# Mixer of a two-layer encoder: rows of ones and gates beside q and k placed by DMA, and q and k taken out of PSUM in one pass

## Chip, core and metric

The kernel runs on one core of a Trainium2 chip. The metric is the time of one execution on the device in microseconds (us), median of three runs; lower is better. The profiled execution is a run of its own. PE is TensorE, ACT is ScalarE, DVE is VectorE, POOL is GpSimd, and SP is the engine that issues most DMAs.

## What is computed

The reference is an encoder trunk of two layers over 256 time steps of 1024 features, in float32. Each layer is a half-step SwiGLU feed-forward network (FFN), a mixer, and a second FFN. What matters here is the attention branch of the mixer:

```python
h = rms_norm(x, g_mix[l]);  z = h @ w_in[l]            # z holds q, k, v, f_logit, gates, ...
qn = rms_norm(q, g_q)                                   # per head of 64; 16 heads
kn = rms_norm(k, g_k)
cum = cumsum(log_sigmoid(f_logit + b_forget), over time)
s = qn @ kn.T * 64 ** -0.5 + cum[query] - cum[key]      # causal
o = softmax(s) @ v
```

The other branch is a gated linear recurrence (RG-LRU); both are gated, added, multiplied by `w_o` and added to x.

## The kernel before

**Matrix products.** Every large product is done in three passes, because each float32 weight is split into a high part (`whi`, a cast on ACT, line 324) and a low part (`wlo`, a subtraction on DVE, line 333). Weights stream from DRAM in pieces of 512 KB (`raw`, five buffers, issued by SP). One visit of a piece multiplies two slices of 128 rows; for each slice there are three matmuls of 512 columns (lines 364 to 366). The two blocks of 128 time steps (`tok` 0 and 1) are worked off one after the other, so an accumulator of 128x512 is complete after eight slices, 24 matmuls.

**Order.** The order of all instructions is fixed when the program is built. A planner `S` keeps a clock of planned time for each engine and a list of chains (generators). After each slice, which it counts as 3 x (512/2400 + 0.0027) = 0.648 us, it calls a hook in which chains whose due time has come put their next instructions into the engines' queues. `yield t, "d"` means: not before planned time t, unless DVE's own planned clock is already further. On the chip each engine executes its queue strictly in order and waits on semaphores. POOL's queue holds the few POOL operations and POOL's DMA issues.

**PSUM.** There are two x banks, two y banks and four z banks. A big product of the mixer takes its accumulator from the x banks (`xbank`), transposes and scores use z banks, and the attention output uses y banks.

**q and k.** The 16 heads are in two halves (`hf`), and each half has a block for q (`w` = 0) and one for k (`w` = 1), in the order q0, k0, q1, k1. When an accumulator is complete, `ev_qk` scales it by the row's inverse norm into `nat` in SBUF (`scale_any`, line 459 on DVE or 462 on ACT, whichever the planner holds to be free sooner) and squares it on ACT (line 1029). `qk_chain` then reduces the squares per head on DVE (line 874), takes the power -1/2 on POOL (line 878), multiplies `nat` by it on DVE (line 881), transposes the result on PE (`quad`, line 448) and scales it into the tile `qk[w, hf]`.

**Extra rows.** That tile has two planes (`e`, even and odd heads) of 128 partitions. In each plane 64 partitions hold the head's features; two groups of 32 of the other 64 hold extra features, so that one matmul of 128 rows gives the scores with the gate terms added. One group selects the head with ones (`new_qk`, a POOL copy of a part of the identity matrix, line 901), the other holds the cumulated gates `cum` (`bias_chain`, copies on DVE, line 308, or ACT, line 311). A group of ones in the tile of q meets a group of gates in the tile of k, and the other way round.

**Attention.** `att_chain` starts eight pairs of heads, at most two at a time. It starts pairs 0 to 3 when the four chains of half 0 are over and `bias_chain(0)` has been planned, and pairs 4 to 7 likewise for half 1. A pair does its scores on PE (line 934), masks and takes minima on DVE (line 950), exponentials on ACT (line 959), scaling (lines 459 and 462), transposes (line 448), copies out of PSUM (lines 308 and 311), and the product with v (line 992). All this is woven between the matmuls of k0, q1, k1 and the gate blocks.

Of the kernel before, what the change touches and what calls it, by code (L numbers as in the profile page):

```python
# [8 lines left out]
F32 = mybir.dt.float32  # L9
F32R = mybir.dt.float32r  # L10
AF = mybir.ActivationFunctionType
ALU = mybir.AluOpType
AX = mybir.AxisListType

P = 128
D = 1024
KD = D // P
T = 256
# [4 lines left out]
DH = 64  # L23
# [128 lines left out]
def act_c(n, ap=0):  # L152
    return 0.11 + 0.000833 * n + 0.093 * ap


def dve_c(n):
    return 0.09 + 0.00104 * n
# [3 lines left out]
def hybrid_encoder_kernel(  # L161
# [6 lines left out]
    nc = tc.nc  # L168
    S = Sched()
# [7 lines left out]
    tmp_p = ctx.enter_context(tc.tile_pool(name="tmp", bufs=NTMP))  # L177
    att_p = ctx.enter_context(tc.tile_pool(name="att", bufs=NLIVE))
    sm_p = ctx.enter_context(tc.tile_pool(name="sm", bufs=2))
    ps_x = ctx.enter_context(tc.tile_pool(name="ps_x", bufs=2, space=bass.MemoryType.PSUM))  # L180
    ps_y = ctx.enter_context(tc.tile_pool(name="ps_y", bufs=2, space=bass.MemoryType.PSUM))
    ps_z = ctx.enter_context(tc.tile_pool(name="ps_z", bufs=4, space=bass.MemoryType.PSUM))
# [3 lines left out]
    def nm(s):  # L186
        cnt[0] += 1
        return f"{s}_{cnt[0]}"

    def new(pool, shape, tag, dt=F32):  # L190
        return pool.tile(shape, dt, tag=tag, name=nm(tag))

    nat_ring, z_ring, y_ring, tmp_ring = [], [], [], []

    def new_nat(n=512):
        r = S.claim(nat_ring, NNAT)
        return new(nat_p, [P, n], "nat"), r

    def new_tmp(shape=None):
        r = S.claim(tmp_ring, NTMP)  # L200
        return new(tmp_p, shape or [P, 512], "tmp"), r

    def bank(pool, tag):
        return pool.tile([P, 512], F32, tag=tag, name=nm(tag))
# [11 lines left out]
    def slot(shape, dt=F32):  # L216
        i = free_slots.pop(0)
        t = slot_p.tile(shape, dt, tag=f"s{i}", name=nm(f"s{i}"))
        return [t, i]

    def free(s):
        free_slots.append(s[1])
        s[0] = None
# [4 lines left out]
    def bc(ap, n):  # L228

        return ap.unsqueeze(2).to_broadcast([ap.shape[0], ap.shape[1], n])  # L230
# [72 lines left out]
    def copy_any(out_, in_, n, dep, fast=False):  # L303

        a = max(S.t["a"], dep, S.now) + act_c(n)
        d = max(S.t["d"], dep, S.now) + dve_c(n if not fast else n // 2)
        if d < a:
            nc.vector.tensor_copy(out_, in_)
            S.t["d"] = d
        else:  # L310
            nc.scalar.copy(out_, in_)
            S.t["a"] = a
        return min(a, d) + LAT
# [65 lines left out]
    def take(n):  # L379
        i = hpos[0]  # L380
        hpos[0] += n
        return i

    def block(lhs, evac, pool, ncol=512, norm=None, mixed=False):

        nk = 1024 // ncol
        n = KD // nk
        i0 = take(n)
        accs = {}
        order = [(tok, i) for tok in range(NT) for i in range(n)]  # L390
        if mixed:
            order = [(tok, i) for i in range(n) for tok in range(NT)]
        for tok, i in order:
            if i == 0:
                a, r = pool()
                accs[tok] = a[:, :ncol], r
            acc, r = accs[tok]

            def fin():
                evac(tok, acc)  # L400
                r.free = True

            if norm is not None:
                norm.before(tok, i * nk)
            visit(i0 + i, acc, lhs, i * nk, tok, i == 0, i == n - 1, fin if i == n - 1 else None)


    ident = const.tile([P, P], F32, name="ident")
# [45 lines left out]
    def scale_any(out_, in_, scale, n, fast=False):  # L454

        a = max(S.t["a"], S.now) + act_c(n, 1)
        d = max(S.t["d"], S.now) + dve_c(n if not fast else n // 2)
        if d < a:
            nc.vector.tensor_scalar(out=out_, in0=in_, scalar1=scale, scalar2=None, op0=ALU.mult)
            S.t["d"] = d  # L460
        else:
            nc.scalar.activation(out_, in_, AF.Copy, scale=scale)
            S.t["a"] = a
        return min(a, d) + LAT
# [80 lines left out]
    def rs(tok):  # L545
        return rstd[:, tok:tok + 1]

    def xbank():
        r = Rec()
        return bank(ps_x, "x"), r  # L550


# [61 lines left out]


    fw = {}

    def load_fw(l):
        r, rr = new_tmp([P, KD, H])
        nc.sync.dma_start(out=r, in_=w_in[l, :, OFF_F:OFF_F + H].rearrange("(k p) n -> p k n", p=P))  # L620
        w = const.tile([P, KD, 2 * H], F32R, tag="fw", name=nm("fw"))
        fw[l] = w
        yield S.now + 8.0, "a"
        nc.scalar.copy(w[:, :, :H], r)
        yield S.use("a", 0.4), "d"
        nc.vector.tensor_tensor(out=w[:, :, H:], in0=r, in1=f32(w[:, :, :H]), op=ALU.subtract)
        S.use("d", 0.3)
        rr.free = True
# [25 lines left out]
    def mix(l, nrm):  # L654
        lhs = nrm.lhs()
# [81 lines left out]
        cum = att_p.tile([P, T], F32, tag="cum", name=nm("cum"), bufs=1)  # L737
# [130 lines left out]
        qk = {}  # L868
        qk_c = {0: [], 1: []}

        def qk_chain(w, hf, tok, nat, sq, dep):
            yield dep, "d"
            rq = sm_p.tile([P, 8], F32, tag="rq", name=nm("rq"), bufs=4)
            nc.vector.tensor_reduce(out=rq, in_=sq[0].rearrange("p (h d) -> p h d", d=DH), axis=AX.X, op=ALU.add)
            sq[1].free = True
            nc.vector.tensor_scalar(out=rq, in0=rq, scalar1=1.0 / DH, scalar2=EPS, op0=ALU.mult, op1=ALU.add)
            d = S.use("d", dve_c(512) + 0.1)
            nc.gpsimd.tensor_tensor(out=rq, in0=rq, in1=mhalf, op=ALU.pow)
            yield d + POW, "d"
            n3 = nat[0].rearrange("p (h d) -> p h d", d=DH)  # L880
            nc.vector.tensor_tensor(out=n3, in0=n3, in1=bc(rq, DH), op=ALU.mult)
            yield S.use("d", dve_c(512)), "p"
            ps, rz = zbank()
            quad(nat[0], ps)
            nat[1].free = True
            gcol = gqm[:, l:l + 1] if w == 0 else col(R_GK)
            for e in range(2):
                yield S.now, "d"
                b = slice(e * DH, e * DH + DH)
                scale_any(qk[w, hf][0][b, e, :, tok * P:(tok + 1) * P], k4(ps)[b], gcol[b], 512)  # L890
            rz.free = True

        def quarters(w):

            return [(e, slice(r, r + 32), slice(r ^ 32, (r ^ 32) + 32)) for e, r in ((0, 64 + 32 * w), (1, 32 * w))]

        def new_qk(w, hf):
            t = qk[w, hf] = slot([P, 2, KD // 2, T])
            for e, one, _ in quarters(w):
                c0 = one.start + hf * 8 + e  # L900
                nc.gpsimd.tensor_copy(t[0][one, e], bc(ident[one, c0:c0 + 7:2], T))

        def bias_chain(hf):
            for w in range(2):
                for e, _, acc in quarters(w):
                    yield S.now, "d"
                    n = KD // 2
                    copy_any(qk[w, hf][0][acc, e], cum[acc].unsqueeze(1).to_broadcast([32, n, T]), n * T, S.now, True)


        OT = {}
# [109 lines left out]
        for hf in range(2):  # L1021
            for w in range(2):
                new_qk(w, hf)

                def ev_qk(tok, acc):
                    nat = new_nat()
                    scale_any(nat[0], acc, rs(tok), 512)
                    sq = new_tmp()
                    nc.scalar.activation(sq[0], acc, AF.Square, scale=rs(tok))
                    dep = S.use("a", act_c(512, 1))  # L1030
                    c = S.add(qk_chain(w, hf, tok, nat, sq, dep), dep, "d")
                    nat[1].user = sq[1].user = c
                    S.step(c)
                    qk_c[hf].append(c)
                block(lhs, ev_qk, xbank)
            if hf == 0:
                att = S.add(att_chain(), S.now, "p", True)

# [2 lines left out]
        for gi in range(2):  # L1041
            g = slot([P, NT, D])
            gates.append(g)
            for hf in range(2):
                c0 = gi * D + hf * 512
# [86 lines left out]
    def rows_chain():  # L1132
        yield 20.0, "p"
        for l in range(L):
            load_rows(l)
        yield S.now + 70.0, "p"
        for l in range(L):
            ps, rz = zbank()
            nc.tensor.transpose(ps[:, :NROW], rows[:, l, :], ident[:NROW, :NROW])
            yield S.use("p", 0.12), "d"  # L1140
            nc.vector.tensor_copy(cols[:, l, :], ps[:, :NROW])
            nc.vector.tensor_scalar(out=gqm[:, l:l + 1], in0=cols[:, l, R_GQ:R_GQ + 1], scalar1=-(DH ** -0.5),
                                    scalar2=None, op0=ALU.mult)
            S.use("d", 0.3)
            rz.free = True
        free(rows_s)
        yield from load_fw(0)

    def program():
# [75 lines left out]
```

## Time and profile before

| | |
|---|---|
| median of 3 runs | 1305.29 us (1305.26 to 1306.33) |
| the profiled execution: its own time | 1305.66 us |
| its span, first to last instruction | 1303.9 us |
| PE busy | 1287.2 us (99%) |
| DVE / ACT / POOL busy | 815.5 / 706.5 / 84.8 us |
| granted TensorE clock, mean | 1.000 of full speed |

Times in the rows are microseconds from the first instruction unless marked ns. A matmul's record lasts from its issue to the modelled end of its pipeline, so matmuls of 0.39 us overlap and follow each other every 0.23 us. In a timeline, "x4" means four instructions merged, and the bracket gives the idle time of the engine before the row and what ended it. A helper's line stands for all its callers: line 448 is every group of transposes.

### The profile page before, as it was taken

The page shows a single profiled execution, that of the slowest core. Times are in us where ns is not written, and L with a number is a line of the kernel's source. Part 1 is how long each engine was busy: PE and PEld are TensorE (multiplying, and loading weights), DVE is VectorE, ACT ScalarE, POOL GpSimd, SP SyncE. Part 2 cuts the span into 40 slices and gives each one's busy share as a digit, 9 for nine tenths or more (in the row PEclk, how much of TensorE's full clock was granted, in tenths as well). Part 3 has the DMA queues.
Part 4 walks back from the last instruction along what each step waited for, and adds up shares of the span by engine and source line. Part 5 has one row for each costly group of instructions (what it writes and reads, how often), then busy time and mean ns, then how long its engine had stood idle before and what let it go on. Part 6 is the DMA issues. An engine that isn't in the chain of part 4 may idle for free.

```text
span 1303.9 us, 16570 instructions
## 1 busy us (share of the span) xinstructions
PE 1287.2 (99%) x6209; PEld 1065.9 (82%) x6209; DVE 815.5 (63%) x1131; ACT 706.5 (54%) x988; POOL 84.8 (7%) x85
## 2 busy tenths in 40 slices
PE   8999999999999999999999999999999999999998
PEld 6888888887778888888888888888877788888887
DVE  5655558799765666555575555678987567655553
ACT  6544446776865455444454444558768554544442
POOL 5000001005100000000000000000250000000000
PEclk9999999999999999999999999999999999999999
DMA  8655557365446565555565565574654455555551
GB/s 273 198 188 184 181 161 217 123 191 154 118 142 201 181 194 194 184 182 183 162 208 183 192 194 182 156 212 126 181 146 145 145 195 172 189 190 192 192 186 59
DMA packets 128896, 229.92 MB, mean 176 GB/s; under 512 B 9848, under 2 KB 22320, under 8 KB 128816
## 3 DMA queue, kind: packets, MB, share of 16 engines
q1 hardware_dynamic: 127968, 228.75, 55.6%
q8 instruction: 49, 0.80, 0.2%
q0 software_dynamic: 832, 0.11, 0.1%
q14 instruction: 31, 0.25, 0.1%
q10 hardware_dynamic: 16, 0.00, 0.0%
HBM read 227.78 MB, written 1.05 MB: 175 GB/s over the span
## 4 chain that ended last, share of the span: by engine, by line
PE 91%; DVE 6%; ACT 1%; issue 1%; DMA 1%; SPq 0%; DVEq 0%; ACTq 0%
PE x L364 13%; PE x L365 13%; PE x L366 13%; PE z L364 12%; PE z L366 12%; PE z L365 12%; PE z L448 4%; PE y L364 3%; PE y L366 3%; PE y L365 3%; DVE wlo L333 2%; PE z L934 1%; PE z L762 1%; PE y L992 1%; DVE s L824 1%
## 5 line engine op out<-in xcount | busy, mean ns | idle before, releaser
L333 DVE TENSOR_TENSOR wlo<-raw,whi 128x1024 fp32r<-128x1024 f32 x424 | 515.9, 1226 | 251.2 <-ACT whi L324 243.2
L324 ACT CAST whi<-raw 128x1024 fp32r<-128x1024 f32 x424 | 442.4, 1050 | 319.9 <-PE z L366 136.8
L364 PE MATMUL x<-whi,s 128*128 128x512 f32 x832 | 337.3, 405 | 1.5 <-ACT whi L324 1.3
L365 PE MATMUL x<-wlo,s 128*128 128x512 f32 x832 | 325.3, 391 | 1.9 <-DVE wlo L333 1.1
L366 PE MATMUL x<-whi,s 128*128 128x512 f32 x832 | 325.3, 391 | 0.1
L364 PE MATMUL z<-whi,s 128*128 128x512 f32 (+1 forms) x752 | 282.5, 376 | 0.0
L366 PE MATMUL z<-whi,s 128*128 128x512 f32 (+1 forms) x752 | 279.7, 372 | 0.0
L365 PE MATMUL z<-wlo,s 128*128 128x512 f32 (+1 forms) x752 | 279.6, 372 | 0.0
L366 PEld LDWEIGHTS x<-whi,s 128*128 128x128 f32 x832 | 156.3, 188 | 34.1 <-DVE s L471 0.5
L364 PEld LDWEIGHTS x<-whi,s 128*128 128x128 f32 x832 | 156.5, 188 | 33.7 <-issue 2.1
L365 PEld LDWEIGHTS x<-wlo,s 128*128 128x128 f32 x832 | 156.7, 188 | 32.4 <-DVE wlo L333 2.0
L366 PEld LDWEIGHTS z<-whi,s 128*128 128x128 f32 x752 | 141.8, 189 | 24.9
L365 PEld LDWEIGHTS z<-wlo,s 128*128 128x128 f32 x752 | 141.9, 189 | 23.7
L364 PEld LDWEIGHTS z<-whi,s 128*128 128x128 f32 x752 | 141.8, 189 | 23.7
L589 ACT ACTIVATE nat<-z,rstd 128x512 f32<-128x512 f32 (+1 forms) x46 | 30.0, 653 | 77.7 <-PE z L366 77.6
L364 PE MATMUL y<-whi,s 128*128 128x512 f32 x176 | 71.0, 403 | 0.0
L366 PE MATMUL y<-whi,s 128*128 128x512 f32 x176 | 68.9, 391 | 0.0
L365 PE MATMUL y<-wlo,s 128*128 128x512 f32 x176 | 68.7, 391 | 0.0
L594 DVE SCALAR_TENSOR_TENSOR nat<-z,rstd,nat 128x512 f32<-128x512 f32 (+1 forms) x48 | 33.8, 704 | 54.2 <-PE z L366 54.2
L469 ACT CAST s<-z 128x512 fp32r<-128x512 f32 (+1 forms) x56 | 31.1, 555 | 66.9 <-PE z L448 66.5
L501 POOL TENSOR_TENSOR rstd<-msum,mhalf 128x1 f32<-128x1 f32 x12 | 11.8, 985 | 819.4 <-ACT whi L324 524.5
L471 DVE TENSOR_TENSOR s<-z,s 128x512 fp32r<-128x512 f32 (+1 forms) x56 | 36.4, 650 | 29.7 <-ACT s L469 29.7
(152 smaller groups left out, 933.7 us busy)
## 6 DMA issues: line engine op xcount, KB each, us to landing
raw<-in_w_up_dram SPq DMA_DIRECT2D x176, 512.0 KB, 4.6
raw<-in_w_in_dram SPq DMA_DIRECT2D x112, 512.0 KB, 4.3
raw<-in_w_down_dram SPq DMA_DIRECT2D x88, 512.0 KB, 4.4
raw<-in_w_lru_out_dram SPq DMA_DIRECT2D x16, 512.0 KB, 4.7
raw<-in_w_attn_out_dram SPq DMA_DIRECT2D x16, 512.0 KB, 4.7
raw<-in_w_o_dram SPq DMA_DIRECT2D x16, 512.0 KB, 5.3
tmp<-in_b_gate_dram SPq DMA_DIRECT2D x8, 256.0 KB, 4.9
xn<-in_x_dram SPq DMA_DIRECT2D x4, 256.0 KB, 4.6
```

The lines of the kernel that those rows point to most:

```text
L324: nc.scalar.copy(hi, raws[i])
L333: nc.vector.tensor_tensor(out=lo, in0=raws.pop(i), in1=f32(hi), op=ALU.subtract)
L364: nc.tensor.matmul(acc, lhsT=lhs(0, k0 + kk)[:, ts], rhs=hi[:, kk, :], start=st, stop=False)
L365: nc.tensor.matmul(acc, lhsT=lhs(0, k0 + kk)[:, ts], rhs=lo[:, kk, :], start=False, stop=False)
L366: nc.tensor.matmul(acc, lhsT=lhs(1, k0 + kk)[:, ts], rhs=hi[:, kk, :], start=False, stop=sp)
L448: nc.tensor.transpose(dst_ps[:, j * P:(j + 1) * P], src[:, j * P:(j + 1) * P], ident)
L469: nc.scalar.copy(hi, t)
L471: nc.vector.tensor_tensor(out=lo, in0=t, in1=f32(hi), op=ALU.subtract)
L589: nc.scalar.activation(s[tok][0], acc, AF.Silu, scale=rs(tok))
L594: nc.vector.scalar_tensor_tensor(out=h, in0=acc, scalar=rs(tok), in1=h, op0=ALU.mult, op1=ALU.mult)
L762: nc.tensor.matmul(ps[:, g, :], lhsT=wax[0][:, g, n, :], rhs=xr[0][:, n, :], start=True, stop=True)
L824: nc.vector.tensor_tensor_scan(t_[:, n, :], r[:, n, :], i_[:, n, :], 0.0, ALU.mult, ALU.add)
```

## The change

The POOL copies of ones become DMA loads, issued by POOL, from two images (`ones_d`) in DRAM; these are built once, at the end of the chain that prepares constants in the first FFN (`ones_chain`). The copies of gate rows become DMAs from the tile `cum`, issued by POOL, and the chain lets 3.0 us of planned time pass. The scaling into `nat` in `ev_qk` is dropped; `qk_chain` keeps the accumulator's PSUM bank until the power is there, and one DVE instruction multiplies by both factors on the way out. The banks become a ring of two records (`x_ring`), so that the planner knows when a bank is held; k of half 0 takes the y banks.

```diff
--- before.py
+++ after.py
@@ -177,6 +177,7 @@
     tmp_p = ctx.enter_context(tc.tile_pool(name="tmp", bufs=NTMP))
     att_p = ctx.enter_context(tc.tile_pool(name="att", bufs=NLIVE))
     sm_p = ctx.enter_context(tc.tile_pool(name="sm", bufs=2))
+    dram = ctx.enter_context(tc.tile_pool(name="dram", bufs=1, space=bass.MemoryType.DRAM))
     ps_x = ctx.enter_context(tc.tile_pool(name="ps_x", bufs=2, space=bass.MemoryType.PSUM))
     ps_y = ctx.enter_context(tc.tile_pool(name="ps_y", bufs=2, space=bass.MemoryType.PSUM))
     ps_z = ctx.enter_context(tc.tile_pool(name="ps_z", bufs=4, space=bass.MemoryType.PSUM))
@@ -190,7 +191,8 @@
     def new(pool, shape, tag, dt=F32):
         return pool.tile(shape, dt, tag=tag, name=nm(tag))
 
-    nat_ring, z_ring, y_ring, tmp_ring = [], [], [], []
+    nat_ring, z_ring, y_ring, x_ring, tmp_ring = [], [], [], [], []
+    held = [None]
 
     def new_nat(n=512):
         r = S.claim(nat_ring, NNAT)
@@ -397,8 +399,8 @@
             acc, r = accs[tok]
 
             def fin():
-                evac(tok, acc)
-                r.free = True
+                held[0] = r
+                r.free = evac(tok, acc) is None
 
             if norm is not None:
                 norm.before(tok, i * nk)
@@ -546,7 +548,7 @@
         return rstd[:, tok:tok + 1]
 
     def xbank():
-        r = Rec()
+        r = S.claim(x_ring, 2)
         return bank(ps_x, "x"), r
 
 
@@ -614,6 +616,26 @@
 
 
     fw = {}
+    ones_d = [dram.tile([P, 2, KD // 2, T], F32, name=f"ones_d{hf}") for hf in range(2)]
+
+    def quarters(w):
+
+        return [(e, slice(r, r + 32), slice(r ^ 32, (r ^ 32) + 32)) for e, r in ((0, 64 + 32 * w), (1, 32 * w))]
+
+    def ones_chain():
+
+        for hf in range(2):
+            t = slot([P, 2, KD // 2, T])
+            for w in range(2):
+                for e, one, _ in quarters(w):
+                    c0 = one.start + hf * 8 + e
+                    yield S.now, "a"
+                    nc.scalar.copy(t[0][one, e], bc(ident[one, c0:c0 + 7:2], T))
+                    S.use("a", act_c(4 * T))
+            for e in range(2):
+                b = slice((1 - e) * DH, (2 - e) * DH)
+                nc.gpsimd.dma_start(out=ones_d[hf][b, e], in_=t[0][b, e])
+            free(t)
 
     def load_fw(l):
         r, rr = new_tmp([P, KD, H])
@@ -868,7 +890,7 @@
         qk = {}
         qk_c = {0: [], 1: []}
 
-        def qk_chain(w, hf, tok, nat, sq, dep):
+        def qk_chain(w, hf, tok, acc, r, sq, dep):
             yield dep, "d"
             rq = sm_p.tile([P, 8], F32, tag="rq", name=nm("rq"), bufs=4)
             nc.vector.tensor_reduce(out=rq, in_=sq[0].rearrange("p (h d) -> p h d", d=DH), axis=AX.X, op=ALU.add)
@@ -877,8 +899,11 @@
             d = S.use("d", dve_c(512) + 0.1)
             nc.gpsimd.tensor_tensor(out=rq, in0=rq, in1=mhalf, op=ALU.pow)
             yield d + POW, "d"
-            n3 = nat[0].rearrange("p (h d) -> p h d", d=DH)
-            nc.vector.tensor_tensor(out=n3, in0=n3, in1=bc(rq, DH), op=ALU.mult)
+            nat = new_nat()
+            h3 = lambda t: t.rearrange("p (h d) -> p h d", d=DH)
+            nc.vector.scalar_tensor_tensor(out=h3(nat[0]), in0=h3(acc), scalar=rs(tok), in1=bc(rq, DH), op0=ALU.mult,
+                                           op1=ALU.mult)
+            r.free = True
             yield S.use("d", dve_c(512)), "p"
             ps, rz = zbank()
             quad(nat[0], ps)
@@ -890,22 +915,16 @@
                 scale_any(qk[w, hf][0][b, e, :, tok * P:(tok + 1) * P], k4(ps)[b], gcol[b], 512)
             rz.free = True
 
-        def quarters(w):
-
-            return [(e, slice(r, r + 32), slice(r ^ 32, (r ^ 32) + 32)) for e, r in ((0, 64 + 32 * w), (1, 32 * w))]
-
         def new_qk(w, hf):
             t = qk[w, hf] = slot([P, 2, KD // 2, T])
             for e, one, _ in quarters(w):
-                c0 = one.start + hf * 8 + e
-                nc.gpsimd.tensor_copy(t[0][one, e], bc(ident[one, c0:c0 + 7:2], T))
+                nc.gpsimd.dma_start(out=t[0][one, e], in_=ones_d[hf][one, e])
 
         def bias_chain(hf):
             for w in range(2):
                 for e, _, acc in quarters(w):
-                    yield S.now, "d"
-                    n = KD // 2
-                    copy_any(qk[w, hf][0][acc, e], cum[acc].unsqueeze(1).to_broadcast([32, n, T]), n * T, S.now, True)
+                    nc.gpsimd.dma_start(out=qk[w, hf][0][acc, e], in_=cum[acc].unsqueeze(1).to_broadcast([32, KD // 2, T]))
+            yield S.now + 3.0, "d"
 
 
         OT = {}
@@ -1023,16 +1042,16 @@
                 new_qk(w, hf)
 
                 def ev_qk(tok, acc):
-                    nat = new_nat()
-                    scale_any(nat[0], acc, rs(tok), 512)
+                    r = held[0]
                     sq = new_tmp()
                     nc.scalar.activation(sq[0], acc, AF.Square, scale=rs(tok))
                     dep = S.use("a", act_c(512, 1))
-                    c = S.add(qk_chain(w, hf, tok, nat, sq, dep), dep, "d")
-                    nat[1].user = sq[1].user = c
+                    c = S.add(qk_chain(w, hf, tok, acc, r, sq, dep), dep, "d")
+                    r.user = sq[1].user = c
                     S.step(c)
                     qk_c[hf].append(c)
-                block(lhs, ev_qk, xbank)
+                    return c
+                block(lhs, ev_qk, ybank if w > hf else xbank)
             if hf == 0:
                 att = S.add(att_chain(), S.now, "p", True)
 
@@ -1144,6 +1163,7 @@
             S.use("d", 0.3)
             rz.free = True
         free(rows_s)
+        yield from ones_chain()
         yield from load_fw(0)
 
     def program():
```

## Rows read from the trace of the kernel before

**Rows 1.** Page, part 1: busy us, share of the span, instructions per engine.
```profile
span 1303.9 us, 16570 instructions
...
PE 1287.2 (99%) x6209; PEld 1065.9 (82%) x6209; DVE 815.5 (63%) x1131; ACT 706.5 (54%) x988; POOL 84.8 (7%) x85
```

**Rows 2.** Stretches of the first mixer: us, busy us per engine, PEclk, DMA share, GB/s.
```profile
285.00:303.00 18.00, 17.12 (x81) 13.94 (x80) 17.90 (x22) 13.58 (x17) 7.98 (x5) 1.00 0.63 179
303.00:329.00 26.00, 24.25 (x118) 19.84 (x117) 21.95 (x46) 18.49 (x35) 14.25 (x8) 1.00 0.50 146
329.00:357.00 28.00, 26.58 (x155) 20.34 (x154) 22.04 (x54) 24.34 (x56) 4.19 (x2) 1.00 0.42 123
...
312.50:314.70 2.20, 0.47 (x3) 0.06 (x2) 2.09 (x5) 2.15 (x3) 1.41 (x1) 1.00 0.16 61
```

**Rows 3.** Waits of PE: us in total, times, longest us.
```profile
PE z L934 <- DVE s L308: 3.5, 2, 1.7
```

**Rows 4.** Timeline around the first stall: start, us, engine, line, operation, [idle before].
```profile
295.90 1.23 DVE L333 TENSOR_TENSOR wlo<-raw,whi 128x1024 fp32r<-128x1024 f32 x1
...
297.55 3.60 POOL L901 COPY s<-ident 32x1024 f32<-32x1024 f32 x2
...
298.18 2.06 DVE L333 TENSOR_TENSOR wlo<-raw,whi 128x1024 fp32r<-128x1024 f32 x1
...
301.83 0.63 PE L448 MATMUL z<-ident,nat 128*128 128x128 f32 x4 [0.88 <-DVE nat L881]
```

**Rows 5.** Timeline around the second stall.
```profile
310.97 0.60 PE L448 MATMUL z<-ident,nat 128*128 128x128 f32 x4
...
312.28 0.67 DVE L874 TENSOR_REDUCE rq<-tmp 128x8 f32<-128x512 f32 x1
...
313.18 2.10 DVE L308 COPY s<-cum 32x1024 f32<-32x1024 f32 x3
313.29 2.07 POOL L878 TENSOR_TENSOR rq<-rq,mhalf 128x8 f32<-128x8 f32 x1 [0.88 <-DVE rq L876]
...
314.71 1.61 PE L934 MATMUL z<-s,s 128*128 128x128 f32 x8 [1.75 <-DVE s L308]
```

**Rows 6.** Timeline of the third stall and of half 1.
```profile
340.85 1.64 POOL L878 TENSOR_TENSOR rq<-rq,mhalf 128x8 f32<-128x8 f32 x1 [6.77 <-DVE rq L876]
...
350.24 0.55 PE L448 MATMUL z<-ident,pr 128*128 128x128 f32 x3 [1.11 <-ACT pt L311]
...
353.72 1.47 PE L934 MATMUL z<-s,s 128*128 128x128 f32 x8
```

**Rows 7.** Groups of instructions by shape: busy us, mean ns | idle before.
```profile
L311 ACT COPY s<-cum 32x1024 f32<-32x1024 f32 x6 | 6.3, 1043 | 0.1
```

**Rows 8.** POOL's DMA issues, lines 439 and 434: ns min/median/max; issue to landing.
```profile
L439 POOL DMA_DIRECT2D bfb<-in_b_forget_dram x2: 573/573/573, 26.4 to 33.7; - x2
...
DMA to landing us min/median/max: 3.2/3.8/5.2
```

**Rows 9.** Timeline: the bank's chain in half 1.
```profile
325.84 1.64 POOL L878 TENSOR_TENSOR rq<-rq,mhalf 128x8 f32<-128x8 f32 x1 [7.07 <-DVE rq L876]
...
327.04 0.75 DVE L459 TENSOR_SCALAR nat<-x,rstd 128x512 f32<-128x512 f32 x1 [1.34 <-PE x L366]
...
329.96 0.69 DVE L881 TENSOR_TENSOR nat<-nat,rq 128x512 f32<-128x512 f32 x1
```

**Rows 10.** Page, part 6: DMA issues, KB each, median us to landing.
```profile
out_dram<-xn SPq DMA_DIRECT2D x4, 256.0 KB, 2.0
```

**Rows 11.** Chain that ended last, in order of time: start, us, what.
```profile
302.46 0.23 PE x L364
```

**Rows 12.** Stretches after PE's last matmul, columns as in rows 2.
```profile
1300.00:1301.00 1.00, 0.20 (x1) 0.00 (x0) 0.69 (x1) 0.00 (x0) 0.00 (x0) 1.00 0.00 0
...
1303.00:1303.90 0.90, 0.00 (x0) 0.00 (x0) 0.00 (x0) 0.00 (x0) 0.00 (x0) 0.63 0.00 0
```

**Rows 13.** Timeline of PE at the start.
```profile
1.43 2.39 PE L1162 MATMUL x<-ident 128*128 128x128 f32 x10 [1.43 <-POOL ident masks.py:199]
```

## Prediction

> **What bounds the kernel now.** I read the page first: TensorE (PE) is busy in 99% of the span [rows 1]. So the kernel can only gain where PE stands still, 1303.9 - 1287.2 = 16.7 us in all. Next came the table of stretches, to see where that is: in the first mixer PE is idle for 0.88, 1.75 and 1.42 us in three neighbouring stretches, 4.05 us together [rows 2], and the second layer repeats it. The other 8.6 us lie at the start and the end, far from the change. That gives a ceiling: an edit that removed every mixer stall would save 2 x 4.05 = 8.1 us, 0.6%. VectorE (DVE) is busy 17.9 of 18 us in the first of these stretches and looks like the bound, but PE is busy in 17.12 of the same 18. Work taken from DVE or ScalarE (ACT) counts only through those three stalls.
>
> The list of waits names what PE waited for, each entry twice, once per layer; the longest is the first scores behind the copies of the gate rows [rows 3]. The timelines show why each stall happens.
>
> *First stall.* While GpSimd (POOL) copies the rows of ones (line 901), a DVE subtraction that took 1.23 us just before takes 2.06. The multiplication of line 881 behind it ends late, and PE waits 0.88 us for it [rows 4].
>
> *Second stall.* After the last transposes of half 0 (at 310.97), DVE reduces the next block's squares, then makes three of the four gate-row copies; POOL takes the power for that next block at 313.29. The scores were next on PE at 314.71 - 1.75 = 312.96 and start at 314.71 [rows 5].
>
> *Third stall.* Transposes wait 1.11 us for an ACT copy out of PSUM [rows 6], which stands in ACT's queue behind softmax scalings and a weight cast.
>
> **The change, part by part, per layer.**
>
> *Rows of ones.* Eight POOL copies, 3.6 us for the pair in the first stall [rows 4], become eight POOL DMA issues. An issue of 128 pieces takes 0.57 us [rows 8], a pair 1.1, and nothing in these rows shows an issue slowing DVE. The first stall goes: -0.88 us (bounds -0.88, and 0 if issues hold DVE as copies do). The source in DRAM is made once, by eight ACT copies of 32x1024, 8 x 1.04 = 8.3 us [rows 7], in the first FFN; ACT is idle 46% of the span [rows 1], so nothing. Without that cover each would delay a weight cast by up to 1.04 us, 8.3 once. The traffic is some 5 MB on DMA engines that are busy 63% at most in the three stretches [rows 2].
>
> *One pass out of PSUM.* Eight scalings (0.75 us on DVE) disappear; the multiplication now reads PSUM and does both, for which I take the 0.75 of the scaling in place of its own 0.69 [rows 9]. That frees 8 x 0.75 - 8 x 0.06 = 5.5 us of DVE and ACT, worth something only in the third stall.
>
> *Gate rows.* Eight copies, about 0.7 us on DVE and 1.04 on ACT [rows 5, 7], become eight POOL DMAs, and the code lets 3.0 us of planned time pass before the scores may be issued. When do the four issues of half 0 run? POOL executes in program order, and the power of the next block (line 878) is ahead of them: the reduction that feeds it stands before the copies on DVE [rows 5]. It ends at 313.29 + 2.07 = 315.36, 4.4 us after the transposes began. The third issue (k, even heads) is the last that the first score needs and starts 4.4 + 2 x 0.57 = 5.5 us after them. The trace shows no such transfer. The nearest are small POOL DMAs into SBUF with the DMA engines full, 3.2/3.8/5.2 us from issue to landing [rows 8], and 256 KB out of SBUF on idle engines, 2.0 [rows 10]. DMA is only 16% busy around this stall [rows 2], so I take 2.7, nearer the low end; bounds 2.0 and 5.2. Landing: 8.2 us after the transposes began (7.5 to 10.7).
>
> When does PE ask? Before the change, 2.0 us after them. The 3.0 planned us are 3.0/0.648 = 4.6 steps of three matmuls (the code counts 0.648 for one), and a step takes 3 x 0.23 = 0.69 us [rows 11]: 3.2 more. So PE asks at 5.2, a step earlier or later by where the planner's hook falls, and waits 8.2 - 5.2 = 3.0 us where it waited 1.75: +1.25 (bounds 7.5 - 5.9 - 1.75 = -0.1 and 10.7 - 4.5 - 1.75 = +4.5). Everything on PE is late behind it, since PE executes in order.
>
> The Trainium skill, "DMA: Bandwidth & Descriptors", section "Anatomy of one DMA — SWDGE (gpsimd) path", fits a DMA issued by POOL as about 2.0 us plus its bytes over 436 GB/s, so 2.3 us for 128 KB. By that estimate the wait would be 2.6 and the sum 0.8 us lower over both layers; no row here shows a transfer of this kind.
>
> In half 1 the same four issues have no power left ahead of them: the last one starts at 340.85 and takes 1.64, and the scores of half 1 begin at 353.72 [rows 6]. The issues need only the slot and the gate rows, so they land at about 342.5 + 3 x 0.57 + 2.7 = 346.9: hidden by some 7 us of PE work. If that cover were gone, they would cost what half 0 does.
>
> *Third stall.* With DVE free of its scalings, more softmax scalings go there from ACT. I count 1.0 of the 1.42 us in this stretch as gained (0 to 1.42).
>
> *Held banks.* A bank now stays occupied through square, reduction, power and multiplication. Two x banks alternate, and the y banks serve only k of half 0, so at four places (half 1 and the first gate block) an accumulation waits if the chain of the bank's last user outlasts the accumulation between. Tight is the second block of half 1: in the trace the power ends at 325.84 + 1.64 = 327.48, and with 0.75 for the product the bank would be free at 328.2, while the accumulation between is done by 327.04 [rows 9]. PE would wait 1.2 there; at the other places the accumulation between shares PE with scores and products and lasts longer. Less DVE work ahead shortens the chain: I take +0.8, bounds 0 and 3.6 (the product ended at 329.96 + 0.69 = 330.65).
>
> *Sum.* -0.88 + 1.25 - 1.0 + 0.8 = +0.17 per layer, +0.3 for two. The profiled execution took 1305.66 us (span 1303.9 and 1.8 around it), so 1306.0; the median of the runs is 0.4 below that execution: **1305.6**. All low ends give 2 x (-0.88 - 0.1 - 1.42) = -4.8, all high ends 2 x (4.5 + 3.6) = +16.
>
> **Rivals.**
>
> *A: the scores don't wait.* If the planner places the four issues ahead of that power, they run some 4 us earlier and are there in time. Then -0.88 - 1.75 - 1.0 + 0.8 = -2.8 per layer, -5.7 in all: 1299.6. For it: the planner's order hangs on due times that all move a little. Against: the reduction and power are planned before the gate rows now, and no edit moves them behind. Chance 0.24.
>
> *B: the clock falls in the stall (slower).* At the end of the kernel, where PE's last work is over at 1300.2, the granted clock still stood at 1.00 in the first microsecond and averaged 0.63 in the last 0.9, while stalls of up to 1.75 us left it at 1.00 [rows 2, 12]. A fall comes about 3 us into an idle stretch, as long as the forecast wait. At the lower of the two levels (1.2 GHz) PE works half as fast: at the start ten transposes took 2.39 us, 0.24 each, against 0.15 [rows 5, 13]. If it lasts about as long as the idle stretch, 3 us, it loses 1.5 us; with a wait of 3.5, past the point, that is +2.0 per layer: 1305.6 + 4.0 = 1309.6. Against: 3.0 is just short of it. Chance 0.15.
>
> The Trainium skill, "TensorE: Matmul & The Clock Gate", section "What's actually happening", says the same of an idle array: half the clock, and back after it has been busy. By that rule, the trace agrees.
>
> *C: late landing or long-held banks.* Landing after 3.8 us, the median with full engines, adds 1.1 per layer (1307.8); a bank wait of 2.0 instead of 0.8 adds 1.2 (1308.0); both, 1310.2. For it: reduction and product wait in DVE's queue behind subtractions of 1.2 us. Against: DVE loses over 5 us of work. Chance 0.21.
>
> **Numbers.** The forecast has 0.40, with a range of its own from 1303 to 1308. A measurement here tells about 0.2%, 2.6 us, from no change: 1302.7 to 1307.9 counts as the same. A lies on the faster side, B and most of C on the slower; the forecast spills little: faster 0.26, same 0.40, slower 0.34. To leave out no more than two in ten the range takes in A's time and B and C with one bound more: 1299.5 to 1311.
>
> **What would show it.** Right: subtractions at 1.2 us throughout the mixer; PE waiting about 3 us for a gate-row DMA before the first scores of each layer and not at the fifth head pair; the four issues after the power on POOL; no wait of 0.88 us before transposes. Wrong: scores released by something else; a granted clock under 1.00 inside the mixer; PE waiting over 2 us for the product at the start of an x accumulation; idle time of PE in a mixer well off 4.2 us.

## Result and the profile after

The changed kernel takes **1314.47 us** (median of 6 runs, 1314.18 to 1315.44) where the kernel before takes 1305.28 beside it (6 runs, 1304.72 to 1306.33): a ratio of 1.0071, interval 1.0061 to 1.0081. It is 0.7% slower. The forecast of 1305.6 and its range to 1311 both missed, on the slow side.

The profiled execution took 1314.18 us against 1305.66 before. Its page, part 1, has the columns of [rows 1]:

```profile
span 1312.1 us, 16582 instructions
...
PE 1289.5 (98%) x6209; PEld 1067.7 (81%) x6209; DVE 806.4 (61%) x1121; ACT 700.6 (53%) x974; POOL 79.1 (6%) x105
```

The span grew by 8.2 us. PE stood still for 1312.1 - 1289.5 = 22.6 us instead of 16.7, which is +5.9, and was busy for 2.3 us more with the same 6209 matmuls, so part of them ran slower. DVE lost 9.1 us of work, ACT 5.9 and POOL 5.7, and nothing of that shows in the time.

The list of PE's waits (us in total, times, longest) tells where it stood. The entry of [rows 3], 3.5 us for DVE copies, has this in its place:

```profile
PE z L953 <- DMA s<-cum: 12.4, 5, 5.5
...
PE z L450 <- DVE nat L904: 1.5, 2, 0.7
```

The scores (now line 953) wait for the gate-row DMAs, 12.4 us in all. The same three stretches as in [rows 2] show that the first stall has shrunk from 0.88 to 0.73 us, the second has grown from 1.75 to 5.52, and the third, 1.42 us, is gone. The granted clock is no longer 1.00 throughout:

```profile
285.00:303.00 18.00, 17.27 (x81) 14.06 (x80) 17.30 (x23) 12.48 (x15) 7.58 (x5) 1.00 0.62 183
303.00:329.00 26.00, 20.48 (x91) 16.33 (x89) 16.36 (x34) 12.34 (x15) 10.63 (x12) 0.87 0.70 201
329.00:357.00 28.00, 28.00 (x161) 21.94 (x160) 19.07 (x51) 19.78 (x54) 5.50 (x6) 1.00 0.36 100
```

The timeline of the second stall answers to [rows 5]:

```profile
310.46 0.60 PE L450 MATMUL z<-ident,nat 128*128 128x128 f32 x4
...
311.77 0.67 DVE L896 TENSOR_REDUCE rq<-tmp 128x8 f32<-128x512 f32 x1
...
312.79 1.66 POOL L900 TENSOR_TENSOR rq<-rq,mhalf 128x8 f32<-128x8 f32 x1 [3.45 <-DVE rq L898]
...
314.42 2.26 POOL L926 DMA_DIRECT2D s<-cum  x4
...
321.11 1.62 PE L953 MATMUL z<-s,s 128*128 128x128 f32 x4 [5.23 <-DMA s<-cum]
...
323.02 1.62 PE L953 MATMUL z<-s,s 128*128 128x128 f32 x4 [0.29 <-DMA s<-cum]
```

The order is the one forecast: transposes at 310.46, reduction, power on POOL, then the four issues at 314.42. PE runs dry at 321.11 - 5.23 = 315.88. The first scores need the third issue, at about 315.6, and start at 321.11: 5.5 us from that issue to use. The view of the issuing lines, from 310 to 320 us, gives how long transfers took from issue to landing (lowest, median, highest), first for the gate rows, then for the weight pieces that SP issues:

```profile
L926 POOL DMA_DIRECT2D s<-cum x4: 550/556/615, 314.4 to 316.1; - x4
...
DMA to landing us min/median/max: 2.3/5.4/6.8
```

```profile
L302 SPq DMA_DIRECT2D raw<-in_w_in_dram x3: 368/368/368, 314.9 to 317.8; - x3
...
DMA to landing us min/median/max: 4.8/6.8/7.0
```

The first gate-row transfer landed in 2.3 us, as estimated, and the later ones took 5 to 7. Three weight pieces of 512 KB are issued in the same 3 us. Stretches inside the stall (columns as in [rows 2]) show what the DMA engines and the clock did:

```profile
316.00:318.00 2.00, 0.00 (x0) 0.00 (x0) 2.00 (x4) 1.54 (x2) 0.68 (x2) 1.00 0.89 168
...
315.88:319.17 3.29, 0.00 (x0) 0.00 (x0) 2.71 (x5) 1.62 (x2) 1.20 (x3) 1.00 0.94 210
319.17:321.11 1.94, 0.00 (x1) 0.04 (x1) 0.00 (x0) 0.00 (x0) 1.94 (x3) 0.50 1.03 303
321.11:325.99 4.88, 4.58 (x13) 3.32 (x14) 1.96 (x9) 0.00 (x0) 0.36 (x1) 0.50 0.72 211
325.99:330.00 4.01, 4.01 (x23) 3.47 (x22) 2.42 (x10) 3.46 (x7) 0.00 (x0) 1.00 0.44 131
```

The DMA engines are 89% to 100% busy while the gate rows are on their way. In the trace of before they were nearly idle where the forecast placed the four issues (315.4 to 317.1), but 75% busy in the 2.1 us behind these, in which the transfers would have been under way:

```profile
315.40:317.10 1.70, 1.70 (x10) 1.48 (x10) 1.70 (x2) 0.01 (x1) 1.68 (x1) 1.00 0.04 10
317.10:319.20 2.10, 2.10 (x13) 1.85 (x12) 2.00 (x10) 1.78 (x2) 1.61 (x2) 1.00 0.75 201
```

And the clock: 3.29 us after PE's last matmul the granted clock goes from 1.00 to 0.50 (from 2.4 to 1.2 GHz) and comes back at 325.99, 4.88 us after PE resumed. Layer 2 repeats it: PE idle from 963.70, the clock at 0.50 from 967.70, 4.00 us later, for another 6.83 us.

### The profile page after: what moved, and what is told of

Read it like the earlier page. It is cut to its first block, busy times and chain, and to the rows that moved or that the text cites. A ratio compares the mean times of both kernels' runs of the same rounds, so it can differ in the third digit from the quotient of the medians.

```text
span 1312.1 us, 16582 instructions
## 1 busy us (share of the span) xinstructions
PE 1289.5 (98%) x6209; PEld 1067.7 (81%) x6209; DVE 806.4 (61%) x1121; ACT 700.6 (53%) x974; POOL 79.1 (6%) x105
## 4 chain that ended last, share of the span: by engine, by line
PE 92%; DVE 3%; DMA 2%; POOL 1%; issue 1%; ACT 0%; SPq 0%; DVEq 0%; POOLq 0%
PE x L366 13%; PE x L368 13%; PE x L367 13%; PE z L366 12%; PE z L368 12%; PE z L367 12%; PE z L450 4%; PE y L366 3%; PE y L368 3%; PE y L367 3%; PE z L953 2%; DMA s<-cum 2%; PE z L784 1%; DVE wlo L335 1%; PE y L1011 1%
## 5 line engine op out<-in xcount | busy, mean ns | idle before, releaser
L366 PE MATMUL x<-whi,s 128*128 128x512 f32 x800 | 324.8, 406 | 1.6 <-ACT whi L326 1.6
L367 PE MATMUL x<-wlo,s 128*128 128x512 f32 x800 | 312.8, 391 | 1.9 <-DVE wlo L335 1.1
L368 PE MATMUL x<-whi,s 128*128 128x512 f32 x800 | 313.0, 391 | 0.1
L368 PEld LDWEIGHTS x<-whi,s 128*128 128x128 f32 x800 | 150.5, 188 | 33.1 <-DVE s L473 0.5
L366 PEld LDWEIGHTS x<-whi,s 128*128 128x128 f32 x800 | 150.6, 188 | 32.5 <-ACT whi L326 1.9
L367 PEld LDWEIGHTS x<-wlo,s 128*128 128x128 f32 x800 | 150.8, 189 | 31.5 <-DVE wlo L335 1.9
L366 PE MATMUL y<-whi,s 128*128 128x512 f32 x208 | 83.7, 403 | 0.0
L368 PE MATMUL y<-whi,s 128*128 128x512 f32 x208 | 81.3, 391 | 0.0
L367 PE MATMUL y<-wlo,s 128*128 128x512 f32 x208 | 81.1, 390 | 0.0
```

Of the source, the lines that this page charges most:

```text
L366: nc.tensor.matmul(acc, lhsT=lhs(0, k0 + kk)[:, ts], rhs=hi[:, kk, :], start=st, stop=False)
L367: nc.tensor.matmul(acc, lhsT=lhs(0, k0 + kk)[:, ts], rhs=lo[:, kk, :], start=False, stop=False)
L368: nc.tensor.matmul(acc, lhsT=lhs(1, k0 + kk)[:, ts], rhs=hi[:, kk, :], start=False, stop=sp)
```

## The experiments

The theory: the whole loss lies in the gate rows, because their transfers land late, and because PE then idles long enough for the clock to fall. The rivals: the held banks and the one-pass product lose the time; the DMAs of the ones do; or the planned wait of 3.0 us puts the scores in a bad place whatever the transfers do. Each kernel was timed beside the kernel before.

### Which part loses the time

**The change with gate rows by copies again.**

```
 def bias_chain(hf):
     for w in range(2):
         for e, _, acc in quarters(w):
-            nc.gpsimd.dma_start(out=qk[w, hf][0][acc, e], in_=cum[acc]...)
-    yield S.now + 3.0, "d"
+            yield S.now, "d"
+            n = KD // 2
+            copy_any(qk[w, hf][0][acc, e], cum[acc]..., n * T, S.now, True)
```

> The changed kernel with one part undone: the gate rows are copied by DVE and ACT again, the ones stay DMA loads and q and k still leave PSUM once. Theory G (the whole loss is PE's wait for the gate-row DMAs and the clock that falls in it): no wait for a DMA, the scores wait about 1.7 us for the copies as before, the granted clock stays at 1.00; about 2.4 us of idle PE time per layer instead of 4.05, so 1302 (1300 to 1304.5). Rival H (held banks or the loads of ones cost as well): 1307 or more.

Measured: 1305.36 us, ratio 1.0001 (0.9992 to 1.0011). Undoing this one part takes back all 9 us, but the kernel is not faster than before, though I had expected 1302 from two stalls removed. The waits of PE from 285 to 360 us and the timeline say why:

```profile
PE z L954 <- ACT whi L326: 1.7, 1, 1.7
PE x L366 <- ACT pr L979: 1.4, 1, 1.4
PE z L450 <- DVE nat L904: 0.7, 1, 0.7
PE z L954 <- PE y L1012: 0.6, 1, 0.6
```

```profile
325.36 1.66 POOL L900 TENSOR_TENSOR rq<-rq,mhalf 128x8 f32<-128x8 f32 x1 [9.50 <-DVE rq L898]
...
327.06 0.75 DVE L904 SCALAR_TENSOR_TENSOR nat<-x,rstd,rq 128x512 f32<-128x512 f32 x1
...
327.96 0.47 PE L366 MATMUL x<-whi,s 128*128 128x512 f32 x1 [1.44 <-ACT pr L979]
```

The list puts the second wait down to an ACT operation, but the accumulation into an x bank starts 0.15 us after the product of line 904 has left that bank (327.06 + 0.75 = 327.81). It is the held bank, at the second block of half 1, where the prediction looked for it: 1.44 us. The 0.7 us before the transposes are a wait for the new product, in the place of the first stall. The last line is new as well: the fifth pair's scores start at 352.30, right behind three gate-row copies on DVE (350.11 to 352.19). With the 1.7 us of the second stall that makes 4.5 us of idle PE time per layer, where before had 4.05.

**Before, with only the gate rows by DMA** (its `bias_chain` replaced by the changed one).

> The kernel before with the gate rows by DMA as the only edit (ones copied by POOL, q and k scaled into SBUF first). Theory G: this one part brings the whole loss, a wait of 5 us or more before the first scores of each layer and a granted clock of 0.5 for some microseconds: 1314 (1311 to 1317). Rival H: under 1309, the rest of the loss being in the other parts.

Measured: 1313.83 us, ratio 1.0070 (1.0055 to 1.0085). One part gives the whole loss. Its waits from 285 to 360 us:

```profile
PE z L933 <- DMA s<-cum: 5.7, 2, 5.3
PE z L448 <- DVE nat L881: 0.9, 1, 0.9
```

The clock is at 0.50 for 6.83 us in both layers here too. The gate rows landed in 2.4/5.5/7.0 us, again with three weight pieces issued beside them (315.2 to 318.1), so the pieces don't come from the one pass.

**Before, with only the ones by DMA** (`ones_d`, `ones_chain` and the DMA in `new_qk`).

> The kernel before with the ones by DMA as the only edit. The prediction's term: POOL's copies no longer slow DVE, the first stall of 0.88 us per layer goes, 1303.5 (1302 to 1304.5). Rival P (the product of line 881 is late for another reason too, since 0.73 us of this stall is left in the changed kernel): 0.6 us or more of the stall stays, 1304.7 or more.

Measured: 1303.69 us, ratio 0.9991 (0.9981 to 1.0000). The first stall of [rows 4] is gone. The subtraction keeps its pace, and no wait for the product is left; the gain in time is at the edge of what ten runs show, since the interval reaches 1.0000:

```profile
296.80 1.21 DVE L334 TENSOR_TENSOR wlo<-raw,whi 128x1024 fp32r<-128x1024 f32 x1
...
297.93 0.68 DVE L903 TENSOR_TENSOR nat<-nat,rq 128x512 f32<-128x512 f32 x1
```

**Before, with only the one pass out of PSUM** (held banks, line 904's product; ones and gate rows by copies).

> The kernel before with the one pass out of PSUM as the only edit; both kinds of rows are copied as before. Theory T: the third stall goes, a wait of about 1.4 us for the product that frees a bank comes in half 1, and the first two stalls stay, so the sum is about zero or a loss: 1306.5 (1305 to 1308). Rival U: 1304 or less, the freed 5.5 us of DVE and ACT per layer being a gain.

Measured: 1304.97 us, ratio 0.9999 (0.9990 to 1.0009). It removes the third stall and pays the held bank for it (1.41 us at the same place); the first stall comes out at 0.73, and the fifth pair's scores wait 0.68 us for copies of gate rows. It is worth nothing by itself.

### What makes the transfers late

**The change without the weight pieces at that time.** Eight pieces of the branch-gate weights per layer are not loaded; the casts read x from SBUF in their place, so the branch gates come from other numbers while the work of the engines stays.

```
 src, nk, ncol = hcs[i]
+if 106 <= i % 212 < 114:
+    raws[i] = xn[:, 0, :].rearrange("p (k n) -> p k n", k=nk)
+    return
```

> The changed kernel without the loads of eight pieces of gate weights per layer, the ones in flight around the gate-row DMAs; their casts and subtractions read x in SBUF instead, so the branch gates are computed from other numbers. Theory D (the gate rows land late because the weight pieces share the DMA engines): the four land 2.3 to 3.5 us after their issue instead of 2.3 to 6.8, PE waits about 2.5 us instead of 5.5, the clock stays at 1.00 or nearly; 1304.5 (1302 to 1307). Rival S (POOL's own queue is slow after the first transfer): landings of 5 to 7 us as before, 1312 or more.

Measured: 1303.53 us, ratio 0.9986 (0.9976 to 0.9996). The gate rows' landing from 305 to 325 us and the wait before the first scores:

```profile
DMA to landing us min/median/max: 2.2/2.4/2.7
```

```profile
317.83 1.55 PE L956 MATMUL z<-s,s 128*128 128x128 f32 x8 [2.50 <-DMA s<-cum]
```

With the pieces away the transfers take 2.2 to 2.7 us and the wait is 2.50, near the prediction's 2.7 and 3.0. The weight pieces make the rest. DVE's work beside the issues does not: from 314.0 to 316.5 DVE is busy for all of the 2.50 us in this run too. The profiled execution (1300.96 us, the fastest of ten) kept its clock; executions whose mean clock was 0.995 to 0.997 took 1304.1 to 1305.1, so the fall seems to come sometimes even here, but no trace shows its place in those.

**The four issues from ACT's queue** (`nc.scalar.dma_start` in place of `nc.gpsimd.dma_start`).

> The changed kernel with the four gate-row DMAs issued from ACT's queue instead of POOL's, at the same place of the program. There they don't stand behind the power and use the hardware queue. Theory D (late because they share the DMA engines with weight pieces that start at about 316 us): issued near 312.5, about 2 us earlier, they land before those pieces, in 2.0 to 3 us; PE waits under 1 us, 1300.5 (1299 to 1303). Rival S (the transfer of this shape takes 5 us wherever it is issued): a wait of 2 to 3 us, 1304 to 1308.

Measured: 1301.53 us, ratio 0.9979 (0.9968 to 0.9991). The issues no longer stand behind the power: they run at 311.46 to 313.5, before the weight pieces, and landed in 2.4/2.7/3.2 us in layer 1, where the scores of half 0 wait 0.33 us in all. The scores of half 1 wait for their transfers, 1.25 us in layer 1 and 1.35 in layer 2, though these landed in 2.3 to 2.4. The profiled execution (1305.62) fell back in layer 2, with waits of 0.67 and 2.26 us and the clock low for 6.83 us; of the other nine, six took 1300.0 to 1302.1 and three 1304.8 to 1305.2. The queue and the time of the issues changed together here, so this run does not tell the two apart.

**The planned wait 9.0 in place of 3.0.**

> The changed kernel with 9.0 us of planned time instead of 3.0 between the issue of the gate rows and the scores; nothing else. Theory G (PE simply asks too early; the transfers are fine): PE asks about 6.3 us later with matmuls of the next blocks in between, after the last landing, so no wait for the DMA and clock 1.00 in the mixer: 1299.5 (1298 to 1302). Rival L (the attention starts too late and its end sticks out behind the gate blocks, or pairs crowd): 1303 or more.

Measured: 1300.67 us, ratio 0.9964 (0.9951 to 0.9977). With more work planned ahead of the scores the late transfers (2.4/5.3/8.0 us to land) are covered; what stays per layer is 0.73 us for the product and 0.95 for the held bank. This speaks against the rival that the planned place is bad whatever the transfers do: with the place kept, the run without the weight pieces lost nothing, and with the transfers kept, this one didn't.

### What the clock costs

**PE kept busy in the wait.** Before the first scores PE does 44 transposes of the identity into a bank that nobody reads.

```
 yield S.now, "p"
+if j == 0:
+    wz, rw = zbank()
+    for _ in range(44):
+        nc.tensor.transpose(wz[:, :P], ident, ident)
+    rw.free = True
```

> The changed kernel with 44 transposes of the identity matrix put on PE ahead of the first scores of each layer: work of about 4.8 us that nobody reads, inside the wait of 5.2 us. Theory K (the fall of the clock is a cost of its own, 4.9 us at half rate, 2.4 per layer): granted clock 1.00 throughout the mixer and 4.9 us less, 1309.6 (1308.5 to 1311). Rival W (the wait alone makes the loss, the recorded clock costs nothing): 1314.5 or more.

Measured: 1312.52 us (4 runs, 1310.60 to 1314.24), ratio 1.0054 (1.0039 to 1.0069), between the two expectations. The profiled execution, the fastest of the four, took 1310.60, 3.6 less than that of the change; the slowest had a mean clock of 0.997, and no trace shows where it fell. Its timeline, and the stretch of the wait:

```profile
315.34 4.97 PE L949 MATMUL z<-ident 128*128 128x128 f32 x44
...
320.84 0.89 PE L958 MATMUL z<-s,s 128*128 128x128 f32 x4 [0.54 <-DMA s<-cum]
...
322.87 0.89 PE L958 MATMUL z<-s,s 128*128 128x128 f32 x4 [1.13 <-DMA s<-cum]
```

```profile
315.00:320.30 5.30, 5.30 (x47) 4.93 (x45) 3.20 (x5) 1.90 (x3) 3.21 (x5) 1.00 0.91 227
```

The clock stays at 1.00 and four score matmuls take 0.89 us; in the change, at 0.50, they took 1.62. The landing did not move (2.4/5.5/7.0 us), so most of the wait stays; some of what the clock gives back goes into a longer wait for the last transfer (1.13 in place of 0.29). The clock is thus a minor part and the wait the major one. In sizes, as an estimate: the 4.58 busy us at 0.50 would be 2.3 at full clock, and PE busy grew by 2.3 us over both layers by the pages of the profile; so between 1.2 and 2.3 us per layer.

### A version that is faster

**The change with both rows issued when the tile opens.**

```
 t = qk[w, hf] = slot([P, 2, KD // 2, T])
+S.need(late[0])
-for e, one, _ in quarters(w):
+for e, one, acc in quarters(w):
     nc.gpsimd.dma_start(out=t[0][one, e], in_=ones_d[hf][one, e])
+    nc.gpsimd.dma_start(out=t[0][acc, e], in_=cum[acc]...)
```

`bias_chain` and its planned wait go; `S.need(late[0])` has the planner finish the chain that makes `cum` first.

> The changed kernel with the gate rows' DMAs issued together with the loads of ones, when a tile is opened, far ahead of the power and of the scores (the cumulated gates are there since 254.7 us in the trace), and without the 3.0 us of planned time. Theory G: no wait before the first scores, clock 1.00, about 0.7 us of idle PE time per layer left, 1299 (1297 to 1302). Rival H: the gain stays away, 1304 or more. Rival Q (eight transfers in a row on POOL's queue hold up the powers): the wait moves to the multiplication, 1303 or more.

Measured: 1299.57 us, ratio 0.9956 (0.9941 to 0.9971). All waits of PE from 285 to 360 us:

```profile
PE z L450 <- DVE nat L904: 0.7, 1, 0.7
PE x L366 <- DVE nat L904: 0.4, 1, 0.4
```

**Before, with both rows issued when the tile opens** (the same, without the one pass).

> The kernel before with both kinds of rows loaded by DMA when a tile is opened (as in the run that issues the gate rows early), while q and k are scaled into SBUF first, as before. Theory T (the one pass out of PSUM frees DVE and ACT, but its held banks give the gain back): the first two stalls go and only the third, 1.31 us per layer, stays, so 1299.9 (1298.5 to 1301.3), within 0.1% of the same kernel with the one pass, which keeps 1.18. Rival U (the one pass is worth having once the scores don't wait): 1301.5 or more.

Measured: **1297.58 us**, ratio **0.9944** (0.9929 to 0.9959): the fastest of all, better than expected, in part because the third stall, of which 1.31 us was to stay, came out at 0.72. Its stretches:

```profile
285.00:303.00 18.00, 18.00 (x85) 14.88 (x84) 17.55 (x23) 15.01 (x19) 9.19 (x7) 1.00 0.71 187
303.00:329.00 26.00, 26.00 (x143) 21.09 (x142) 22.23 (x55) 17.33 (x36) 10.15 (x12) 1.00 0.68 198
329.00:357.00 28.00, 27.21 (x146) 21.89 (x145) 22.70 (x56) 19.68 (x53) 4.12 (x2) 1.00 0.45 137
```

Of the 4.05 us of stalls in [rows 2], 0.79 are left. Its gate rows too take long, 4.7/5.2/6.8 us to land; issued this early, nobody waits for them.

**The former of the two again, beside the latter.**

> The early gate rows once more, beside the two others on the same chip: 1299.6 (1298.8 to 1300.6), PE waiting 0.73 and 0.45 us per layer for products of line 904.

Measured: 1299.00 us, ratio 0.9957 (0.9942 to 0.9972). The one pass costs 1.4 us once the scores don't wait. The spans of the two profiled executions differ by 1.2 us: (1.22 - 0.79) + (1.23 - 0.79) = 0.9 us is PE's idle time in the two mixers, and 0.33 us its idle time in the first 100 us, at the load of the first weights. There the two profiled executions of the version with the one pass differ by 0.43 among themselves, so I don't put that part down to the change.

## Why the prediction was wrong

**The step that failed** is the landing of the gate rows: "DMA is only 16% busy around this stall [rows 2], so I take 2.7, nearer the low end". The 16% was read in the trace of before from 312.5 to 314.7, and by the prediction's own times the issues begin at 315.4. Over the time of the transfers the same trace has 75% (317.1 to 319.2), so the row was the wrong one. The change then fills that time further: SP issues three weight pieces, at 314.9, 316.1 and 317.8, just behind the first gate-row issue, and the DMA engines are 89% to 100% busy. From the third issue to its use it took 5.5 us, beyond the high bound of 5.2, which I had named and set aside as full engines. Taking the pieces away brought 2.2 to 2.7.

Before issued one piece in that time, at 316.4. That there are three now can be read from the traces. SP waits for a subtraction to free a `raw` buffer, and each of the three issues stands at the end of one (about 314.9, 316.0 and 317.8). From the changed kernel, the subtractions and SP's waits from 314 to 320 us:

```profile
313.67 2.36 DVE L335 TENSOR_TENSOR wlo<-raw,whi 128x1024 fp32r<-128x1024 f32 x2 [1.03 <-ACT whi L326]
...
316.60 1.22 DVE L335 TENSOR_TENSOR wlo<-raw,whi 128x1024 fp32r<-128x1024 f32 x1
```

```profile
SPq L302 <- DVE wlo L335: 8.5, 3, 6.5
```

Before, DVE made gate-row copies from 313.18 to 315.28 [rows 5], and its next subtraction ended at 316.41. The copies that the change removes had held the weight pieces back, and the prediction has no term for that. No run holds the subtractions back by themselves.

The Trainium skill's estimate of 2.3 us ("DMA: Bandwidth & Descriptors", section "Anatomy of one DMA — SWDGE (gpsimd) path") agrees with the first transfer (2.3) and nearly with those that had no pieces beside them (2.2 to 2.7), and not with the ones that count here (5.4 in the median).

**What stood around it was right.** PE asked 5.42 us after the transposes (forecast 5.2); the power ended 4.0 us after them (4.4), and the issues stood behind it on POOL as said. The wait came out at 5.52 us in layer 1 and 6.42 in layer 2, in place of 3.0.

**The clock**, rival B, came with it, at a price between 1.2 and 2.3 us where B had 1.5. Its point, about 3 us idle, is near the 3.29 and 4.00 us of the changed kernel, but the runs show no fixed point. With only the gate rows by DMA the clock fell 2.4 us into the idle stretch of layer 1; with ACT's queue it fell in layer 2 after 1.5 us of the wait of 2.26, which followed one of 0.67 and 0.89 us of work; and without the weight pieces it stood at 1.00 through 2.50 us in the profiled execution. B's row for the lower level was misread: the trace grants the ten transposes at the start 1.00. What shows the lower level is the four score matmuls, 1.62 us against 0.89. I had priced B with a wait of 3.5 and C with a landing of 3.8, each by itself. One raises the other, since a late landing lengthens the idle stretch in which the clock falls, and I gave the two together no case.

**The sum, over both layers.** Gate rows: +3.77 and +4.67 = +8.4 (forecast +2.5). Clock: +2.3 to +4.6 (0). Third stall: -1.42 per layer (-1.0), plus 0.41 us that the fifth pair waits in layer 2. First stall: -0.15 per layer (-0.88). Held banks: 0 (+0.8 per layer). With the low end for the clock that is 8.4 + 2.3 - 2.8 + 0.4 - 0.3 = +8.0, where the span shows +8.2.

**The ones** were right as a part: alone they end the first stall, as forecast. I did not see that the one-pass product makes a stall of its own there. In the timeline of after the product stands behind a scaling of DVE that itself waited for ACT's:

```profile
296.24 0.76 DVE L461 TENSOR_SCALAR s<-z,gqm 64x512 f32<-64x512 f32 x1 [0.56 <-ACT s L464]
297.03 0.75 DVE L904 SCALAR_TENSOR_TENSOR nat<-x,rstd,rq 128x512 f32<-128x512 f32 x1
...
297.93 0.63 PE L450 MATMUL z<-ident,nat 128*128 128x128 f32 x4 [0.73 <-DVE nat L904]
```

Every traced version with the one pass has this 0.73; the version with the ones alone has not.

**The held bank** was right in place, and in size it depends on what lies ahead: 1.4 us in the second block of half 1 where the scores wait for copies; where they don't, 0.95 at the start of that block (planned wait of 9.0) or 0.4 at the first gate block (rows issued early). The prediction's +0.8 lies in the middle of these. In the changed kernel it is 0. Its scores wait so long that the chain is through by then, but the run with ACT's queue has 0 as well, with a wait of 0.33 us for the scores of half 0, so that may not be the whole reason.

**Half 1** was hidden in layer 1, but barely, and not in layer 2. Its power and its issues ran at 349.31 and 350.89, not near 341, and landed in 2.4/5.1/6.3 us: the third at about 352.0 + 5.1 = 357.1 for scores that start at 358.17. The margin was 1 us and not 7. In layer 2 they landed in 2.4/5.3/6.7 us, and the fifth pair waited 0.41 us.

**Left open:** why some executions of one kernel keep the clock in waits of about 2.5 us and others seem to lose it, and why the held bank costs nothing in the changed kernel.

## What to carry to other kernels

A DMA that replaces a copy is better issued where its inputs are ready, not where the copy stood: here the same transfers cost 9 us behind the last transposes and gain 7.3, together with the ones, when the tile opens (1304.88 to 1297.58). Read the DMA share of the trace of before over the time in which the new transfer would be under way, and not at the wait that it replaces. Ask which prefetches are due to start beside it and which the edit itself sets free earlier, and take the duration with full engines unless none can. Where a forecast wait is about as long as one in which the clock was seen to fall, price the two together.

## What the hardware showed that I had not expected

- Four transfers of 128 KB issued by POOL 0.55 us apart landed in 2.3 us (the first) and 5.4 to 7.7 us (the others, both layers) once weight pieces of 512 KB were issued between them; four with no pieces about took 2.2 to 2.7.
- The granted clock stayed at 0.50 for 6.83 us in both layers, though PE was at work again after 1.94 us in the first. Over the traces it fell between 1.5 and 4.0 us into an idle stretch of PE.
- A wait for a held PSUM bank is put down to whichever operation ended last by the profile: the list named an ACT operation for 1.4 us that the timeline ties to the product reading the bank.
